# One weight load moved behind two others on the SP queue of a hybrid decoder layer

## The chip, the cores and the metric

The kernel runs on one core of a Trainium2 chip. The metric is the device time of one execution in microseconds (us), lower is better. The kernel before has a median of 944.97 us over 3 runs (944.78 to 945.34).

## The reference

One decoder layer over 1024 tokens and 16 meta tokens of width 1024, in float32. The change lies in the feed-forward part, at the seam where the mixing part ends:

```
h = h + rmsnorm(mix @ w_out, g_post_mix)
u = rmsnorm(h, g_pre_ffn)
f = square(relu(u @ w_ff1)) @ w_ff2        # w_ff1 1024 x 4096, w_ff2 4096 x 1024
h = h + rmsnorm(f, g_post_ffn)
```

## The kernel before, in words

All operands of a product are split into a high and a low float32r part, and a product is three matmuls (high by high, high by low, low by high: lines 125, 130 and 131). The high part is a cast on ACT (L96), the low part a subtraction on DVE (L99).

The first feed-forward product, `u @ w_ff1`, is done with fewer block products than the plain one, by sums of weight blocks and sums of token blocks. Its columns are cut into 16 blocks `p` of 256. For each block `prep_a(p)` loads two tiles of 512 KB, `r0` (the upper half of the rows of `w_ff1`) and `r1` (the lower half), makes sums of their quarters with `combine` (L1188, on DVE), and stores the changed `r1` to `s_dram` for later. For block 0, `r1` is a tile of the pool `d` (named d_3559 in the order of instructions) and `r0` one of the pool `raw` (raw_3557). Blocks 2 to 13 take `r1` from the pool `a`.

Four blocks of the upper and four of the lower rows are also loaded ahead of that, two at a time, by `early`: each call issues two loads of 256 KB (`w1_load`, L1185) and splits them. The last of these calls, `early(1, 2, ..., "a")`, loads the tile a_3494, casts it on ACT and subtracts on DVE. Its result is used by `p2(2, ...)` and `p2(3, ...)`, products into the bank `ps_pt`. `early` keeps the name of its second load in `loads[0]`.

The instructions of each engine are put in order by a scheduler when the kernel is built; `behind(name, ins)` adds an order without a wait: `ins` comes later in the stream than the instruction `name`. SP issues nearly all of these loads, and issues them in order: an issue that waits for its tile holds those behind it. Around the change the streams hold, besides: the last of the token rows (`out_norm`, `out_scale`, t = 7: squares on ACT at L1131, the root on POOL at L166 and L172, the scaling on DVE at L1143), their transposes on PE (L1157), and the sums of token blocks (`t_sums`), whose splits `ot2` are operands of the first products of block 0 (`product(ya[p], wa[p][1], ot2, False)`).

Of the kernel before, what the change touches and what calls it, by code (L numbers as in the profile page):

```python
# [37 lines left out]
def hybrid_layer(  # L38
# [19 lines left out]
    def slot(tag, shape, dt=F32):  # L58
        uid[0] += 1
        return slab.tile(shape, dt, tag=tag, name=f"{tag}{uid[0]}", bufs=bufs[tag])  # L60

    def pair(tag, shape):
        return slot(tag, shape, F32R), slot(tag, shape, F32R)
# [17 lines left out]
    def lut(*args, **kwargs):  # L81
        ins = nc.scalar.activation(*args, **kwargs).ins
        if last_lut[0] is not None:
            tc.add_manual_dep(
                ins, last_lut[0],
                mybir.DependencyInfo(
                    mybir.DependencyClass.NoSync, mybir.DependencyReason.DATA
                ),
                reason="lut",
            )  # L90
        last_lut[0] = ins.name
        return ins

    def split(hi, lo, src, eng=None):
        if eng is None:
            cast[0] = nc.scalar.copy(hi, src).ins.name  # L96
        else:
            eng.tensor_copy(hi, src)
        low = nc.vector.tensor_tensor(lo, src, f32(hi), op=ALU.subtract).ins  # L99
        mark[0] = low.name  # L100
        return low
# [4 lines left out]
    def behind(name, *inss):  # L106
        for ins in inss:
            tc.add_manual_dep(
                ins, name,
                mybir.DependencyInfo(  # L110
                    mybir.DependencyClass.NoSync, mybir.DependencyReason.DATA
                ),
                reason="order",
            )
# [924 lines left out]
    for half in range(2):  # L1039
        for c in range(NLRU):  # L1040
            y = ys[c][:, 512 * half : 512 * half + 512]
            ins = lut(y, y, AF.Gelu_apprx_tanh)
# [140 lines left out]
    def w1_load(dst, b, p, a0, a1):  # L1183
        c0 = 256 * p
        return nc.sync.dma_start(dst, w1v[b][:, :, c0 + P * a0 : c0 + P * a1]).ins  # L1185

    def combine(dst, x0, x1, op):
        return nc.vector.tensor_tensor(dst, x0, x1, op=op).ins  # L1188
# [25 lines left out]
    def prep_a(p, late=None):  # L1214
        r0 = slot("raw", [P, 4, 256])
        behind(loads[0], w1_load(r0, 0, p, 0, 2))
        r1 = slot("a" if 2 <= p < 14 else "d", [P, 4, 256])
        w1_load(r1, 1, p, 0, 2)
        a11, a21, a12, a22 = r0[:, :, LO], r0[:, :, HI], r1[:, :, LO], r1[:, :, HI]
        sums = [  # L1220
            combine(a22, a21, a22, ALU.add), combine(a21, a11, a21, ALU.subtract)
        ]
        if late:
            behind(late, *sums)
        hi, lo = pair("ws", [P, 4, 256])
        if p in a11_early:
            split(hi[:, :, HI], lo[:, :, HI], a21)
            first = a11_early[p]
        else:
            split(hi, lo, r0)  # L1230
            first = hi[:, :, LO], lo[:, :, LO]
        combine(a11, a22, a11, ALU.subtract)
        hl = slot("e", [P, 2, 4, P], F32R)
        split(hl[:, 0], hl[:, 1], a11)
        combine(a12, a12, a11, ALU.subtract)
        nc.gpsimd.dma_start(s_dram[p], r1)
        return first, (hl[:, 0], hl[:, 1]), (hi[:, :, HI], lo[:, :, HI])
# [9 lines left out]
    a11_early, a12_early, loads = {}, {}, [None]  # L1247
# [101 lines left out]
    product(y2, a12_early[1], b21, True, kcs=range(2))  # L1349
    t_sums(slice(8, 12))  # L1350
    wa[0] = prep_a(0)
    u2_tiles(7, xns[7])
    product(y2, a12_early[1], b21, True, turned[0], kcs=range(2, 4))
# [7 lines left out]
    for i in range(2):  # L1361
        behind(urgent, split(*map(rows, ot3[i]), t3[i]))
    token_low = mark[0]
    wa[1] = prep_a(1, urgent)


# [14 lines left out]
    for p in range(16):  # L1381
        if p + 2 < 16:
            wa[p + 2] = prep_a(p + 2, None if p else urgent)
        if p >= 13:
            raw_b[p - 13] = fetch_b(p - 13)
        product(ya[p], wa[p][1], ot2, False)
        nc.scalar.copy(block("12", p), ya[p])
        if p == 0:
            p2(3, a12_early[3], last_mm[0])
        if 4 <= p + 2 < 16:  # L1390
            p1(p + 2, wa[p + 2][0])
        product(ya[p], wa[p][2], ot3, False)
        nc.scalar.copy(block("21", p), ya[p])
        if 3 <= p < 9:
            t_rest(p - 3)

        if p == 14:
            ot1 = operand(u2f[1][0:2])
# [337 lines left out]
```

## Time and profile before

| what | value |
|---|---|
| median of 3 runs | 944.97 us (944.78 to 945.34) |
| profiled execution | 945.26 us, of which 943.3 us are the span from the first to the last instruction |
| mean granted TensorE clock | 0.999 of full speed |
| PE busy | 934.0 us, 99% of the span |
| DVE, ACT, POOL busy | 70%, 54%, 14% |
| DMA | 136.49 MB, mean 145 GB/s |
| stretch 311 to 345 us (around the change) | PE 34.00 us busy of 34, DVE 31.95, ACT 26.00, POOL 5.44 |

A row of the timeline has the start in us, the duration in us, the engine, the line, the operation, its tiles and in brackets the idle time ahead of it with what ended that. SPq rows are the issues of DMAs, not the transfers. The rows of the windows give the busy time of PE, of PE's weight load (PEld), of DVE, ACT and POOL, then the granted clock, the DMA share and GB/s.

### The profile page before, as it was taken

The numbers are of one execution on the slowest core, as the hardware profiler recorded it, in microseconds if no ns is written. First come the engines' busy times: TensorE is split into PE (matmuls) and PEld (weight loads), VectorE is DVE, ScalarE is ACT, GpSimd is POOL, SyncE is SP. The second block draws the span as 40 slices with busy tenths as digits, with TensorE's granted clock in tenths as the row PEclk, the third lists the DMA queues.
The fourth block names the chain that finished last, engine by engine and source line by source line (L and its number), as shares of the span: only waits on it lengthen the run. The fifth ranks groups of instructions, "written<-read, shape, count | busy, mean of one in ns | idle before, by whom it ended". The sixth has DMA issues, their size and how long they took to land.

```text
span 943.3 us, 12158 instructions
## 1 busy us (share of the span) xinstructions
PE 934.0 (99%) x4562; PEld 780.8 (83%) x4562; DVE 664.7 (70%) x846; ACT 505.1 (54%) x846; POOL 132.9 (14%) x204
## 2 busy tenths in 40 slices
PE   8999999999999999999999999999999999999997
PEld 7999999877888888888888888888888888888886
DVE  7667788889877986755544465477667676779794
ACT  8546765679434854443655575653533443445441
POOL 4104436430021200110000000001121000001200
PEclk9999999999999999999999999999999999999999
DMA  8220011104359768573422364334777755647934
GB/s 275 58 67 23 24 46 46 46 23 142 101 182 291 234 192 287 180 255 123 157 89 90 116 219 120 103 113 115 198 171 177 210 179 189 191 155 208 242 65 90
DMA packets 99911, 136.49 MB, mean 145 GB/s; under 512 B 24391, under 2 KB 63319, under 8 KB 99853
## 3 DMA queue, kind: packets, MB, share of 16 engines
q1 hardware_dynamic: 90652, 110.67, 36.7%
q0 software_dynamic: 8736, 23.67, 11.8%
q10 hardware_dynamic: 464, 1.38, 0.4%
q8 instruction: 36, 0.59, 0.3%
q14 instruction: 23, 0.18, 0.1%
HBM read 113.60 MB, written 21.50 MB: 143 GB/s over the span
## 4 chain that ended last, share of the span: by engine, by line
PE 98%; DVE 0%; DMA 0%; ACT 0%; issue 0%; DVEq 0%; ACTq 0%
PE ps_acc L125 12%; PE ps_acc L131 11%; PE ps_acc L130 11%; PE ps_pt L130 7%; PE ps_pt L125 7%; PE ps_pt L131 7%; PE ps_s L125 6%; PE ps_s L131 6%; PE ps_s L130 6%; PE ps_o L125 5%; PE ps_o L130 5%; PE ps_o L131 5%; PE ps_o L763 2%; PE ps_acc L988 1%; PE ps_acc L309 1%; PE ps_s L693 1%
## 5 line engine op out<-in xcount | busy, mean ns | idle before, releaser
L99 DVE TENSOR_TENSOR ws<-raw,ws 128x1024 fp32r<-128x1024 f32 (+1 forms) x69 | 83.6, 1212 | 74.3 <-ACT ws L96 23.3
L96 ACT CAST ws<-raw 128x1024 fp32r<-128x1024 f32 (+1 forms) x68 | 69.7, 1026 | 80.8 <-PE ps_o L130 32.6
L96 ACT CAST ws<-e 128x1024 fp32r<-128x1024 f32 x41 | 43.0, 1050 | 84.9 <-PE ps_o L130 37.8
L99 DVE TENSOR_TENSOR b<-b,b 128x1024 fp32r<-128x1024 f32 (+1 forms) x49 | 57.7, 1179 | 27.0 <-PE ps_o L130 21.7
L130 PE MATMUL ps_acc<-a,ws 128*128 128x512 f32 (+3 forms) x224 | 76.3, 341 | 0.0
L125 PE MATMUL ps_acc<-a,ws 128*128 128x512 f32 (+3 forms) x224 | 76.3, 341 | 0.0
L131 PE MATMUL ps_acc<-a,ws 128*128 128x512 f32 (+3 forms) x224 | 75.7, 338 | 0.0
L99 DVE TENSOR_TENSOR ws<-e,ws 128x1024 fp32r<-128x1024 f32 x41 | 50.2, 1224 | 31.2 <-ACT ws L96 17.8
L96 ACT CAST b<-b 128x1024 fp32r<-128x1024 f32 (+1 forms) x49 | 49.5, 1011 | 41.5 <-DVE b L1188 35.3
L750 POOL TENSOR_SCALAR_AFFINE_SELECT c<-c 128x512 fp32r<-128x512 f32 x64 | 51.4, 817 | 75.2 <-ACT c L96 66.1
L131 PE MATMUL ps_acc<-ws,b 128*128 128x512 f32 (+1 forms) x120 | 46.1, 384 | 0.0
L130 PE MATMUL ps_acc<-ws,b 128*128 128x512 f32 (+1 forms) x120 | 46.1, 384 | 0.0
L125 PE MATMUL ps_acc<-ws,b 128*128 128x512 f32 (+1 forms) x120 | 46.0, 385 | 0.0
L125 PEld LDWEIGHTS ps_acc<-a,ws 128*128 128x128 f32 x224 | 42.2, 188 | 3.1 <-DVE b L997 0.3
L131 PEld LDWEIGHTS ps_acc<-a,ws 128*128 128x128 f32 x224 | 42.2, 188 | 3.0
L130 PEld LDWEIGHTS ps_acc<-a,ws 128*128 128x128 f32 x224 | 42.1, 188 | 2.8
L130 PE MATMUL ps_pt<-ws,b 128*128 128x512 f32 x112 | 44.2, 395 | 0.0
L125 PE MATMUL ps_pt<-ws,b 128*128 128x512 f32 x112 | 44.2, 394 | 0.0
L131 PE MATMUL ps_pt<-ws,b 128*128 128x512 f32 x112 | 44.0, 393 | 0.0
L125 PE MATMUL ps_s<-ws,b 128*128 128x512 f32 x110 | 43.4, 395 | 0.0
L130 PE MATMUL ps_s<-ws,b 128*128 128x512 f32 x110 | 43.3, 393 | 0.0
L131 PE MATMUL ps_s<-ws,b 128*128 128x512 f32 x110 | 43.2, 393 | 0.0
(436 smaller groups left out, 2679.8 us busy)
## 6 DMA issues: line engine op xcount, KB each, us to landing
raw<-in_w_ff_dram SPq DMA_DIRECT2D x59, 512.0 KB
e<-in_w_ff_dram SPq DMA_DIRECT2D x43, 512.0 KB
a<-in_w_ff_dram SPq DMA_DIRECT2D x12, 512.0 KB
s_dram<-a POOLq DMA_DIRECT2D x12, 512.0 KB, 3.8
raw<-in_w_in_dram SPq DMA_DIRECT2D x9, 512.0 KB
c<-in_x_dram SPq DMA_DIRECT2D x8, 512.0 KB
d<-in_x_dram SPq DMA_DIRECT2D x8, 512.0 KB
out_dram<-raw SPq DMA_DIRECT2D x8, 512.0 KB
```

Source lines behind the costliest of these rows:

```text
L96: cast[0] = nc.scalar.copy(hi, src).ins.name
L99: low = nc.vector.tensor_tensor(lo, src, f32(hi), op=ALU.subtract).ins
L125: ins = nc.tensor.matmul(dst, lh, rh, start=start, stop=False, skip_group_check=True).ins
L130: nc.tensor.matmul(dst, lh, rl, start=False, stop=False, skip_group_check=True)
L131: last_mm[0] = nc.tensor.matmul(dst, ll, rh, start=False, stop=stop, skip_group_check=True).ins.name
L309: last_mm[0] = nc.tensor.matmul(acc[:, :n], w[k // 2][:, kc, :], u[kc][k % 2][:, t0 : t0 + n], start=k == 0 and kc == 0, stop=k == last an ...
L693: nc.tensor.matmul(dst, q[h][:, c], hi, start=True, stop=False, skip_group_check=True,)
L750: nc.gpsimd.affine_select(out=p_[:, :, s], in_=f32(p_[:, :, 0]), pattern=[[0, 4], [g, P]], compare_op=op, fill=0.0, base=0, channel_multip ...
L763: nc.tensor.matmul(two[:, :, oc : oc + w], v, p_.rearrange("p (j i) s c -> p j (i s c)", j=2)[:, :, pc : pc + w], start=n == 0 and k == 0, ...
L988: ins = nc.tensor.matmul(y2_bank[half], (wh, wh, wl)[k][:, kc, :], (uh, ul, uh)[k][:, t0 : t0 + n], start=m % 24 == 0, stop=m % 24 == 23, ...
```

## The change

In `prep_a`, the load of `r1` for block 0 is put behind `loads[0]`. When block 0 is prepared, that is the second load of the last `early` call. Until now only the load of `r0` was put there, and the scheduler had placed that of `r1` ahead of both early loads.

```diff
@@ prep_a
         r0 = slot("raw", [P, 4, 256])
         behind(loads[0], w1_load(r0, 0, p, 0, 2))
         r1 = slot("a" if 2 <= p < 14 else "d", [P, 4, 256])
-        w1_load(r1, 1, p, 0, 2)
+        ins = w1_load(r1, 1, p, 0, 2)
+        if p == 0:
+            behind(loads[0], ins)
```

On SP, in the stretch after the row of `out_dram` for t = 6, the difference is this (`d_3559` is `r1` of block 0, `a_3494` the early tile in two loads, `raw_3557` is `r0` of block 0):

```order
 L1087 DMA c_2787<-u_dram 128x4x64
 L1129 DMA out_dram<-raw_3333 128x1024
+L1185 DMA a_3494<-in_w_ff_dram 128x4x128 x2
 L1185 DMA d_3559<-in_w_ff_dram 128x4x256
-L1185 DMA a_3494<-in_w_ff_dram 128x4x128 x2
 L1185 DMA raw_3557<-in_w_ff_dram 128x4x256
 L1185 DMA a_3673<-in_w_ff_dram 128x4x256
```

The load of d_3559 now stands behind the two of a_3494, and still ahead of raw_3557. No other row of SP has moved.

On DVE, the instructions that use these loads, and those behind them, stand as before (d_3444 and raw_3446 are the token rows of t = 7):

```order
385 L1128 TENSOR_TENSOR raw_3446<-raw_3446,d_3444 128x1024
386 L99 TENSOR_TENSOR b_3443<-a_3439,b_3442 128x4x2x32
387 L99 TENSOR_TENSOR a_3493<-a_3494,a_3492 128x1024
388 L1188 TENSOR_TENSOR d_3559<-raw_3557,d_3559 128x4x128
389 L1143 TENSOR_SCALAR d_3444<-raw_3446,rs 128x1024
390 L1188 TENSOR_TENSOR raw_3557<-raw_3557 128x4x128
391 L1188 TENSOR_TENSOR a_3436<-c_2786,c_2784 128x256
```

Nothing moved there, nor on PE, ACT or POOL.

## The prediction

> **What bounds the kernel now.** I read the page's busy shares first, then the chain of waits, then who waited for whom on PE, then the windows and the timeline around the moved load.
>
> ```profile
> PE 934.0 (99%) x4562; PEld 780.8 (83%) x4562; DVE 664.7 (70%) x846; ACT 505.1 (54%) x846; POOL 132.9 (14%) x204
> PE 98%; DVE 0%; DMA 0%; ACT 0%; issue 0%; DVEq 0%; ACTq 0%
> PE ps_acc L339 <- DVE base_e L627: 1.5, 1, 1.5
> PE ps_o L401 <- DVE d L248: 1.0, 2, 0.8
> 311.00:345.00 34.00, 34.00 (x160) 27.69 (x159) 31.95 (x53) 26.00 (x54) 5.44 (x8) 1.00 0.63 199
> ```
>
> PE holds 98% of the chain that ended last. Its two waits on the list add up to 2.5 us, both at L339 and L401, which are the warm-up and the first transposes. In the stretch of the change, 311 to 345 us, it is busy for all of 34.00 us. The ends of PE's matmuls are modelled, so a small wait can lie inside a busy row; starts show it.
>
> ```profile
> 312.36 0.39 PE L130 MATMUL ps_acc<-b,a 128*128 128x512 f32 x1
> ...
> 317.47 0.39 PE L131 MATMUL ps_acc<-b,a 128*128 128x512 f32 x1
> ...
> 333.13 0.39 PE L131 MATMUL ps_pt<-b,a 128*128 128x512 f32 x1
> 333.36 0.40 PE L125 MATMUL ps_acc<-b,e 128*128 128x512 f32 x1
> ...
> 342.39 0.39 PE L130 MATMUL ps_s<-b,e 128*128 128x512 f32 x1
> 342.66 0.50 PE L131 MATMUL ps_acc<-b,e 128*128 128x512 f32 x1
> 342.99 0.40 PE L125 MATMUL ps_acc<-b,e 128*128 128x512 f32 x1
> ```
>
> From 312.36 to 317.47 there are 22 steps of 0.232 us each, and 0.23 us also lie between 333.13 and 333.36, where the first product with a weight made from the moved load begins (`e` is the high and low part of the first sum). So nothing waits there. At 342.39 the two steps are 0.27 and 0.33 us, 0.14 us above two regular ones: the one place near the change where PE can have been held up.
>
> **The change, part by part.** Nothing is added or removed; one issue of 512 KB moves behind two of 256 KB on SP. The issues before:
>
> ```profile
> 313.24 0.35 SPq L1129 DMA_DIRECT2D out_dram<-raw  x1
> 313.64 0.43 SPq L1185 DMA_DIRECT2D d<-in_w_ff_dram  x1
> 314.12 1.58 SPq L1185 DMA_DIRECT2D a<-in_w_ff_dram  x2
> 317.99 0.37 SPq L1185 DMA_DIRECT2D raw<-in_w_ff_dram  x1
> ```
>
> The three issues stand one behind the other from 313.64 to 315.70. They still will: the early loads begin at 313.64, and `d` goes out some 1.6 us later, by 315.7. The next issue, `raw`, went out at 317.99, with 2.3 us idle ahead of it. So nothing behind on SP moves, and the two early issues alone move ahead, by 0.48 us (314.12 - 313.64) plus the time that their bytes queued behind those of `d`. That second part is read from the bytes per microsecond:
>
> ```profile
> 314.00:315.00 1.00, 1.00 (x6) 0.82 (x5) 0.95 (x2) 1.00 (x4) 0.00 (x0) 1.00 0.95 365
> 315.00:316.00 1.00, 1.00 (x6) 0.82 (x5) 0.94 (x2) 1.00 (x6) 0.73 (x2) 1.00 0.91 206
> 316.00:317.00 1.00, 1.00 (x6) 0.79 (x5) 0.99 (x3) 0.92 (x4) 1.00 (x2) 1.00 0.97 273
> 317.00:318.00 1.00, 1.00 (x6) 0.82 (x5) 0.56 (x2) 1.00 (x2) 0.56 (x1) 1.00 1.09 359
> 318.00:319.00 1.00, 1.00 (x6) 0.81 (x5) 1.00 (x3) 1.00 (x3) 0.00 (x0) 1.00 1.15 314
> 319.00:320.00 1.00, 1.00 (x6) 0.81 (x5) 1.00 (x3) 0.47 (x1) 0.00 (x0) 1.00 0.70 163
> 320.00:321.00 1.00, 1.00 (x6) 0.81 (x5) 1.00 (x2) 0.89 (x1) 0.00 (x0) 1.00 1.07 375
> ```
>
> One GB/s over 1 us is 1 KB. The write of 524 KB (512 x 1024 bytes) is issued first, then `d`, `a`, `raw`, each 524 KB. In thousands of bytes the sum runs 365, 571, 844, 1203, 1517, 1680, 2055. If they move in the order of issue, the write ends at about 315.8, `d` (1049) at 317.6, `a` (1573) at 319.3 and `raw` (2097) at 321.1. These are estimates. ACT checks them:
>
> ```profile
> 318.85 0.62 ACT L96 CAST b<-a 128x512 fp32r<-128x512 f32 x1
> 320.11 1.05 ACT L96 CAST a<-a 128x1024 fp32r<-128x1024 f32 x1 [0.63 <-DMA a<-in_w_ff_dram]
> 321.06 1.06 ACT L1131 ACTIVATE d<-raw 128x1024 f32<-128x1024 f32 x1
> ```
>
> Its cast of the early tile began at 320.11, after 0.63 us of waiting for that load, which is 0.8 us after the estimated end of its bytes. With the same 0.8 us, the new order lands `a` at 317.6 + 0.8 = 318.4 and `d` at 319.3 + 0.8 = 320.1; `raw`, with the same bytes ahead of it, stays at 321.9.
>
> *The early tile.* ACT is free at 318.85 + 0.62 = 319.47, later than 318.4, so its wait of 0.63 us goes. What is late next is the square of the last token rows (L1131), which needs DVE's sum at L1128:
>
> ```profile
> 319.51 1.22 DVE L1128 TENSOR_TENSOR raw<-raw,d 128x1024 f32<-128x1024 f32 x1
> 321.25 1.22 DVE L99 TENSOR_TENSOR a<-a,a 128x1024 fp32r<-128x1024 f32 x1
> 322.39 0.69 DVE L1188 TENSOR_TENSOR d<-raw,d 128x512 f32<-128x512 f32 x1
> 322.29 0.86 POOL L166 TENSOR_SCALAR ms<-ssq 128x1 f32<-128x1 f32 x1 [4.74 <-ACT d L1131]
> 323.24 0.57 POOL L172 TENSOR_TENSOR rs<-ms,half_pow 128x1 f32<-128x1 f32 x1
> 323.84 0.75 DVE L1143 TENSOR_SCALAR d<-raw,rs 128x1024 f32<-128x1024 f32 x1 [0.77 <-POOL rs L172]
> ```
>
> That sum ends at 319.51 + 1.22 = 320.73, so the square starts 0.33 us earlier at best, and POOL's root and DVE's scaling with it: 0.33 of DVE's idle 0.77 us. DVE then runs nearly without a gap to the instructions that feed PE:
>
> ```profile
> 332.95 0.77 DVE L99 TENSOR_TENSOR b<-a,b 128x256 fp32r<-128x256 f32 x2
> 333.63 0.68 DVE L1308 TENSOR_TENSOR b<-ps_pt,b 128x512 f32<-128x512 f32 x1
> 341.91 0.69 DVE L99 TENSOR_TENSOR e<-raw,e 128x512 fp32r<-128x512 f32 x1
> ```
>
> L1308 adds a result of PE whose last matmul starts at 333.13 and ends at 333.52. DVE begins it at 333.63, so no more than 0.11 us of the 0.33 get past it, and the later `e` at 341.91, whose end (342.60) just precedes PE's 342.66, moves by 0.1 us. The gain at the end is therefore between nothing and the 0.14 us of the two long steps; I take 0.1, the share that passes L1308.
>
> *The moved load.* Its first reader is DVE's sum at 322.39, and that waits for `raw` too, which lands at 321.9 by the same estimate. `d` at 320.1 leaves 2.3 us to the sum and comes ahead of `raw` by 1.8. Cost: nothing, covered by the load of `raw`. If the cover fails and `d` lands after 322.39, DVE stands, with the scaling and the splits for PE's 333.36 behind it; PE had no slack there that I can show (the first of DVE's two splits from 332.95 ends at about 333.34, half of the 0.77 on), so each microsecond would be one at the end. Upper bound within the estimates: all four transfers share the engines and `d` ends with the last at 321.9, still 0.5 us ahead.
>
> A rule that stands against the estimate: the Trainium skill, "DMA: Bandwidth & Descriptors", section "Queues, rings and completion order", says that descriptors of a ring are consumed in order but that completion is not first in, first out. By it `d` could land after `raw`; the 0.63 us of ACT agree with the order of issue, and no run here shows the other case.
>
> *Sum.* The profiled execution took 945.26 us (943.3 of span, 1.96 around it), 0.29 above the median. From its own time the change takes 0.1, to 945.16; from the median, 944.87, rounded to 944.9.
>
> **The rivals.**
>
> *The freed waits reach the end (faster).* If PE's even steps hide waits, the most that this change frees is ACT's 0.63 plus DVE's 0.77 = 1.40 us, giving 943.57; with ACT's alone, 944.34. For it: DVE is busy 31.95 of 34 us and feeds PE to within 0.02 us at 333.36. Against it: PE's steps are as even there as at 312 to 317. Even all of it stays below 0.2% of the time, which is 1.89 us, about what a measurement of this kernel can tell from no change. The Trainium skill's "Perfetto Trace Analysis", section "Identifying the Most-Contended Engine", holds matmul busy time to be a poor measure of headroom and points to the weight load's; by that 34.00 - 27.69 = 6.31 us of this stretch would be open (an estimate), but this trace's even starts don't agree.
>
> *A wait of SP takes hold of the moved issue (slower).* `d` is now the last of three, and SP also waits for older transfers before issues:
>
> ```profile
> SPq L1185 <- DMA out_dram<-raw: 5.0, 3, 2.6
> ```
>
> If `d`'s issue waits w longer than the 315.7 reckoned, `d` lands at 320.1 + w, and `raw`, issued behind it, as much as 1.8 us after that. DVE's sum at 322.39 is then late by 320.1 + w + 1.8 - 322.39 = w - 0.5. It decides from w = 0.5 and passes 0.2% from w = 2.4. At the longest such wait, 2.6 us, the time is 944.97 + 2.1 = 947.1; at all three together, 5.0 us, 949.5. Against it: whatever stood ahead of the third issue before stands there now, and that one was out by 315.70.
>
> *It does not do what it says.* The row of SP has changed, but if the transfers share the engines rather than follow each other, the early tile lands about as before: 944.97.
>
> **How the numbers follow.** Forecast (0.1 us or none) 0.87; freed waits reaching the end 0.06; SP's wait 0.05; shared transfers 0.02. Over 0.2% faster would need more than the 1.40 us that can come free: 0.02, out of the second case. Over 0.2% slower: 0.04 of the third. Within: 0.94. The range: from the fastest run less ACT's wait, 944.78 - 0.63 = 944.1, to the slowest plus a small SP wait (w = 1.6), 945.34 + 1.1 = 946.4.
>
> **What would show it.** In the profile after, the two `a` issues stand first at about 313.6 and `d` third at about 315.2; ACT's wait of 0.63 us for `a` is gone and L1131 starts near 320.75; DVE's wait ahead of L1143 falls from 0.77 to about 0.45; the sum at 322.39 does not move; PE stays at 34.00 of 34 us. I am wrong if DVE waits for a DMA ahead of that sum, if SP has a wait ahead of `d`, or if PE's steps around 333.36 or 342.66 lengthen.

## The result, and the profile after

The changed kernel takes 946.92 us (median of 19 runs, 945.78 to 949.15) where the kernel before takes 945.12 in the same runs: a ratio of 1.0018, 95% interval 1.0012 to 1.0024. So it is some 1.8 us slower. Its profiled execution is one of its quicker ones, 945.99 us with a span of 944.0, which is 0.73 us over the profiled execution of before. (The ratios are estimates of their own, given with their interval, and can differ a little from the quotient of two medians.)

First the page's busy line and chain, then the new line among PE's waits (in us: total, times, longest), then the window from 311 to 345 us:

```profile
PE 934.7 (99%) x4562; PEld 780.8 (83%) x4562; DVE 664.6 (70%) x846; ACT 505.2 (54%) x846; POOL 134.6 (14%) x204
PE 97%; DVE 1%; ACT 0%; DMA 0%; issue 0%; DVEq 0%; ACTq 0%
```

```profile
PE ps_acc L125 <- ACT b L96: 0.2, 1, 0.2
```

```profile
311.00:345.00 34.00, 33.76 (x157) 27.02 (x156) 32.25 (x54) 26.11 (x54) 5.32 (x8) 1.00 0.62 194
```

DVE has come into the chain with 1%, PE has a third wait, and PE is busy for 33.76 of the 34.00 us in which it was busy throughout. Three matmuls fewer fit there (157 for 160). SP's issues in the timeline (here and below, rows that lie between those shown are left out):

```profile
313.91 0.35 SPq L1129 DMA_DIRECT2D out_dram<-raw  x1
314.31 1.32 SPq L1185 DMA_DIRECT2D a<-in_w_ff_dram  x2
315.73 0.63 SPq L1185 DMA_DIRECT2D d<-in_w_ff_dram  x1
318.05 0.37 SPq L1185 DMA_DIRECT2D raw<-in_w_ff_dram  x1
```

The order is the intended one, and `raw` goes out at 318.05, where before had 317.99. The timeline of ACT, then of DVE, where these loads are used:

```profile
319.44 1.04 ACT L96 CAST a<-a 128x1024 fp32r<-128x1024 f32 x1
321.43 1.06 ACT L1131 ACTIVATE d<-raw 128x1024 f32<-128x1024 f32 x1 [0.94 <-DVE raw L1128]
```

```profile
320.18 1.22 DVE L1128 TENSOR_TENSOR raw<-raw,d 128x1024 f32<-128x1024 f32 x1
321.92 1.22 DVE L99 TENSOR_TENSOR a<-a,a 128x1024 fp32r<-128x1024 f32 x1
324.17 0.69 DVE L1188 TENSOR_TENSOR d<-raw,d 128x512 f32<-128x512 f32 x1 [1.03 <-DMA raw<-in_w_ff_dram]
324.78 0.75 DVE L1143 TENSOR_SCALAR d<-raw,rs 128x1024 f32<-128x1024 f32 x1
```

ACT's cast of the early tile has no wait in brackets any more. But the first sum of block 0 now waits 1.03 us for a load, and that load is not the one that was moved: it is `raw`, whose place on the queue is the same. The sum starts at 324.17 instead of 322.39. Ten microseconds later, on DVE and then on PE:

```profile
332.99 0.75 DVE L1188 TENSOR_TENSOR a<-a,c 128x256 f32<-128x256 f32 x2
333.88 0.77 DVE L99 TENSOR_TENSOR b<-a,b 128x256 fp32r<-128x256 f32 x2
```

```profile
333.26 0.40 PE L131 MATMUL ps_pt<-b,a 128*128 128x512 f32 x1
333.90 0.50 PE L125 MATMUL ps_acc<-b,e 128*128 128x512 f32 x1 [0.24 <-ACT b L96]
334.36 0.50 PE L130 MATMUL ps_acc<-b,e 128*128 128x512 f32 x1
334.70 0.39 PE L131 MATMUL ps_acc<-b,e 128*128 128x512 f32 x1
334.93 0.40 PE L125 MATMUL ps_acc<-b,e 128*128 128x512 f32 x1
```

DVE's splits start at 333.88, before they did at 332.95: still 0.93 us late. PE needs 1.67 us from 333.26 to 334.93, four steps that take 0.93 at 0.232 each. The 0.74 lost there is about the whole difference of the two profiled times. The 0.24 in brackets is only part of it: the rest hides in longer rows, since PE's ends are modelled.

So the two ends of the chain are clear, and the experiments have two questions: is DVE's wait what costs the time, and why does `raw` come late.

### The profile page after: what moved, and what is told of

Read it like the earlier page. It is cut to its first block, busy times and chain, and to the rows that moved or that the text cites. A ratio compares the mean times of both kernels' runs of the same rounds, so it can differ in the third digit from the quotient of the medians.

```text
span 944.0 us, 12158 instructions
## 1 busy us (share of the span) xinstructions
PE 934.7 (99%) x4562; PEld 780.8 (83%) x4562; DVE 664.6 (70%) x846; ACT 505.2 (54%) x846; POOL 134.6 (14%) x204
## 3 DMA queue, kind: packets, MB, share of 16 engines
q10 hardware_dynamic: 464, 1.38, 0.5%
## 4 chain that ended last, share of the span: by engine, by line
PE 97%; DVE 1%; ACT 0%; DMA 0%; issue 0%; DVEq 0%; ACTq 0%
PE ps_acc L125 12%; PE ps_acc L130 11%; PE ps_acc L131 11%; PE ps_s L125 6%; PE ps_s L130 6%; PE ps_s L131 6%; PE ps_pt L130 6%; PE ps_pt L125 6%; PE ps_pt L131 6%; PE ps_o L125 5%; PE ps_o L130 5%; PE ps_o L131 5%; PE ps_o L763 2%; PE ps_acc L988 1%; PE ps_acc L309 1%; PE ps_s L693 1%
```

## The experiments

The theories. **A**: `raw` lands late, DVE runs in order, PE gets its operands late. For why `raw` is late: **F**, PE's fetch of its instructions (a 16 KB transfer about every 28 us) meets this load; **C**, the two loads of 512 KB read the same columns of `w_ff1` and get in each other's way; **S**, two loads with wide rows stand directly one behind the other; **T**, there is no spare time between the end of the load ahead and that of `raw`, so a DMA engine that lags does not catch up.

In kernels with added lines the sum L1188 is L1190, L1192 or L1193.

### Both kernels once more

No edit.

> The changed kernel once more. Theory A (late block): the two loads of block 0 land later than DVE can use them, because the moved load now lies directly ahead of raw_3557 in the queue and a lagging DMA engine has no gap in which to catch up. Expected: DVE's sum of block 0 again waits for a DMA, starts past 323.5 us, and PE loses 0.5 to 3 us at the first product of block 0 near 333.4 us; time 946 to 948. Rival B (chance): the late landing of the first profile was one engine's bad luck and the time comes from elsewhere; then the sum starts near 322.4 and PE's loss lies at another place.

> The kernel before once more, for a second profile. Theory A: the sum of block 0 starts without a DMA wait near 322.4 us, PE regular at 333.4; time 945.0. Rival B: the landing of raw_3557 scatters as much as in the changed kernel, with a wait of DVE for it of 1 us or more possible.

The changed kernel: 946.77 us, ratio to before 1.0019 [1.0009, 1.0028]. The kernel before: 945.47, 1.0002 [0.9993, 1.001]. The waits and PE's timeline of the changed one:

```profile
DVE d L1188 <- DMA raw<-in_w_ff_dram: 1.8, 1, 1.8
```

```profile
333.21 0.40 PE L131 MATMUL ps_pt<-b,a 128*128 128x512 f32 x1
334.32 0.50 PE L125 MATMUL ps_acc<-b,e 128*128 128x512 f32 x1 [0.71 <-ACT b L96]
```

It took 946.70, 0.71 more than the first profile of this kernel. DVE's wait is 0.8 longer in it, and PE's step is 1.11 instead of 0.64: the loss grows with the wait. The kernel before was not as theory A expected it, with no wait, but as the rival did: in this second profile of it (945.78), DVE's sum waited 0.52 us, `raw` ended at 323.63 instead of 321.71, and PE's four steps at 333 us lost 0.54 (334.48 - 333.01 less 0.93), where in the first profile they lost nothing. The late load is thus no property of the changed kernel alone.

### Taking work off DVE behind the late load

In both kernels a split and the sum for `s_dram`, which PE doesn't need soon, go behind the last urgent split:

```diff
-            split(hi[:, :, HI], lo[:, :, HI], a21)
+            low = split(hi[:, :, HI], lo[:, :, HI], a21)
-        combine(a12, a12, a11, ALU.subtract)
+        last_sum = combine(a12, a12, a11, ALU.subtract)
+        if p == 0:
+            lazy.extend((low, last_sum))
...
+    behind(urgent, *lazy)
```

> The changed kernel, with two DVE instructions of block 0 that PE does not need before 338.9 us (the low part of ws, and the sum that goes to s_dram; 0.6 us each) put behind the last of the four splits that PE needs at 333.4. Theory A: the loads land as late as before but DVE has 1.2 us in hand, so most of the 1.8 us come back: 945.2 to 946.0. Rival B, and any rival in which the loss is not on DVE's path to 333.4: no gain, 946.5 to 947.3.

> The kernel before with the same two DVE instructions put back. Theory A: DVE's 1.2 us in hand take away what scatter the kernel before had: 944.7 to 945.1, with a narrower spread. Rival: the moved instructions come late for PE at 338.9 or for s_dram, 945.5 or more.

A miss for A, which expected 945.2 to 946.0 and 944.7 to 945.1. With the change 947.52, 1.0026 [1.0017, 1.0035]; before with the same edit 945.78, 1.0006 [0.9997, 1.0015]. The waits with the change:

```profile
DVE d L1188 <- DMA raw<-in_w_ff_dram: 2.2, 1, 2.2
PE ps_acc L131 <- DVE e L99: 1.6, 1, 1.6
PE ps_acc L125 <- ACT b L96: 0.3, 1, 0.3
```

PE's steps at 333 us in the same profile:

```profile
332.95 0.40 PE L131 MATMUL ps_pt<-b,a 128*128 128x512 f32 x1
333.60 0.49 PE L125 MATMUL ps_acc<-b,e 128*128 128x512 f32 x1 [0.26 <-ACT b L96]
334.74 0.39 PE L125 MATMUL ps_acc<-b,e 128*128 128x512 f32 x1
```

The place at 333 us is not cured: the four steps lose 0.86 (334.74 - 332.95 less 0.93), and the 0.3 of the list is only what shows as idle. How much the edit spared there can't be told, since DVE's wait was longer here (2.2). And PE now waits 1.6 at 342.6 for the next operand of DVE (`e`, 0.6 in before with this edit, so that part of this wait comes from the edit itself): work that is taken from in front of one deadline stands in front of the next. The places of the loss fit A, but this pair does not decide for it. Moving these two operations is no remedy.

### PE's fetch of instructions

The profile lists one DMA queue with 36 transfers of instructions and 0.59 MB, 16 KB each. Fifty tiny matmuls in place of a part of the warm-up shift PE's count of instructions, so that the fetch falls at 314.1 us, away from `raw`; the start takes some 3 us longer. In a third kernel eight of them put it inside the transfer of `raw`, in the kernel before.

```diff
-    load(11, 512)
+    load(5, 512)
+    for _ in range(50):
+        nc.tensor.matmul(
+            idle[:16, :16], zeros[:16, :16], zeros[:16, :16], start=True, stop=True,
+            skip_group_check=True,
+        )
```

> The changed kernel with PE's stream of instructions shifted: 6 of the 11 warm-up matmuls at the start give way to 50 tiny ones, so that the transfer that fetches PE's instructions (16384 B, near 322.4 us in every profile so far, in the middle of the loads of block 0) comes some 10 us earlier, near 312 us, where the DMA queues are empty. Theory F (the fetch holds up one DMA engine while it carries raw_3557): raw_3557 lands by 322.5 us on all engines, DVE waits less than 0.3 us, PE loses under 0.3 us at the first product of block 0; the time is that of fetch_before to within 0.3 us, 944.5 to 946.0. Theory S (two wide loads one behind the other, rows of 1024 B without the two narrow loads between them, leave engines behind): as slow against fetch_before as the changed kernel against the kernel before, 1.3 to 2.3 us.

> The kernel before with the same shift, as the base for fetch_after. Both theories: 944.5 to 945.8 us, PE regular at 333.4 (shifted with the start); under theory F with less scatter than before, since now and then the fetch reaches raw_3557 there too.

> The kernel before with the fetch of PE's instructions moved 1.6 us earlier, into the transfer of raw_3557 (one warm-up matmul gives way to 8 tiny ones). Theory F: raw_3557 lands at 323 us or later on one engine, DVE's sum of block 0 waits 0.7 to 2 us, PE loses 0.5 to 1.5 us near 333.4; 945.7 to 947. Theory S: no change, 944.7 to 945.5.

With the change 949.58, 1.0046 [1.0032, 1.0059]; before with the same shift 947.76, 1.0024 [1.0014, 1.0034]. The difference is 1.82 us, as without the shift, and the wait is there without a fetch at `raw`:

```profile
DVE d L1193 <- DMA raw<-in_w_ff_dram: 1.7, 1, 1.7
```

Before with the fetch put at `raw`: 945.48, 1.0009 [1.0001, 1.0018]; DVE's sum came 1 us later:

```profile
323.44 0.69 DVE L1193 TENSOR_TENSOR d<-raw,d 128x512 f32<-128x512 f32 x1 [0.91 <-PE ps_o L1162]
```

(PE's work at L1162 was long done; the load ended at 323.35.) Wait and landing are as F expected, the time is in the other range. A fetch may hold up a load (one profile), but the changed kernel is as late without one: F falls as the cause of the difference. What it adds in single profiles comes up with the landings.

### Other columns, narrower loads

`other_cols` lets the moved load read the columns of block 5, so that block 0's product is of wrong weights. `halves` and `halves_again` issue the moved load as two of half the row width, `upper_halves` does so with `raw`.

```diff
# other_cols
-        ins = w1_load(r1, 1, p, 0, 2)
+        ins = w1_load(r1, 1, p or 5, 0, 2)
# halves, halves_again
...
+            for c in range(2):
+                ins = w1_load(r1[:, :, P * c : P * c + P], 1, p, c, c + 1)
# upper_halves
...
+            for c in range(2):
+                upper = w1_load(r0[:, :, P * c : P * c + P], 0, p, c, c + 1)
```

> The changed kernel with the moved load of 512 KB issued as two of 256 KB, rows of 512 B as in the early loads, in the same place of SP's order. Theory S: raw_3557 lands by 322.5 us as in the kernel before, and the time comes back to 945.0 to 945.5. Theory F: no change, 946.3 to 947.3.

> The kernel with the moved load in two halves once more, for a second profile and a narrower interval; its first profile showed one engine 2.3 us behind on raw_3557 and the first time lay between the two kernels. Theory S: the two engines that lag in every profile of the changed kernel don't lag here, and what was left is a fetch of PE's instructions on one engine; 945.3 to 946.3. Theory C: half of the moved load still lies beside raw_3557, so a lag of about half the size stays, 945.7 to 946.7.

> The changed kernel, in which the moved load reads the columns of block 5 in place of those of block 0 (so block 0's sums are made from another block's lower half); size, place and every instruction are as in the changed kernel. Theory C (the moved load and raw_3557, now adjacent, read the same columns of rows that lie 8 MiB apart in HBM and hinder each other): raw_3557 lands by 322.5 us on all engines, time 945.0 to 945.8. Theory S (adjacent loads with rows of 1024 B, whatever they read): two engines still land raw_3557 1.5 us or more behind the median, time 946.3 to 947.3.

> The changed kernel, with raw_3557 in place of the moved load issued as two loads of 256 KB with rows of 512 B. Theory S: no two wide loads are adjacent, the tile lands by 322.5 us on all engines, 945.0 to 945.8. Theory C: the same rows and columns of HBM are read side by side as before, 946.3 to 947.3.

Other columns: 947.02, 1.0016 [1.0007, 1.0024], as slow as the change; C is not borne out. Its profile caught its quickest execution (945.29), with `raw` on time. Halves: 946.13, 1.0009 [1.0001, 1.0018], and a second time 946.89, 1.0017 [1.0006, 1.0028]. The halves of `raw`: 946.19, 1.0011 [1.0002, 1.002]. Row widths are inconclusive: the three times lie outside all the ranges that were expected, DVE's wait is 1.4 in the first of these profiles, absent in the second, 0.8 in the third, and the 12 executions of `halves_again` fall into five at 945.0 to 945.3 and seven at 946.6 to 950.6 (three of the seven at a granted clock of 0.994 to 0.997, where the others have 0.998 or 0.999). The profiles of `halves` and `halves_again`, and the two of before, show that the same program meets the late load in one execution and not in another.

These kernels also answer the first question, whether DVE's wait costs the time. In `other_cols`, `halves_again` and `upper_halves` the instructions of DVE, ACT and POOL around the change stand as in the changed kernel. DVE's sum and PE's steps in `other_cols`:

```profile
322.97 0.68 DVE L1188 TENSOR_TENSOR d<-raw,d 128x512 f32<-128x512 f32 x1
333.35 0.39 PE L131 MATMUL ps_pt<-b,a 128*128 128x512 f32 x1
333.58 0.40 PE L125 MATMUL ps_acc<-b,e 128*128 128x512 f32 x1
334.28 0.40 PE L125 MATMUL ps_acc<-b,e 128*128 128x512 f32 x1
```

With the changed order and `raw` on time, PE's four steps take 0.93 and the execution is as quick as those of before. The five profiles in order of DVE's wait for `raw` (us):

| profile | DVE's wait | lost in PE's four steps | this execution |
|---|---|---|---|
| `other_cols` | 0 | 0.00 | 945.29 |
| `halves_again` | 0 | 0.02 | 945.25 |
| `upper_halves` | 0.8 | 0.59 | 945.46 |
| changed kernel | 1.0 | 0.74 | 945.99 |
| changed kernel again | 1.8 | 1.21 | 946.70 |

The loss grows with the wait and is gone without it. A is borne out.

### The moved load, earlier

`d_first` keeps the order of before and issues `d` ahead of the write of the token rows of t = 6; `a_first` keeps the order of the change and issues the early tile ahead of that write. There `d` still stands directly in front of `raw`, but goes out at 313.95 instead of 315.73.

```diff
# d_first
-            behind(loads[0], ins)
+            behind(ins.name, outs[6])
...
# a_first
-            behind(loads[0], ins)
+            behind(loads[0], ins, outs[6])
+            behind(outs[6].name, ins)
+            behind(ins.name, upper)
...
```

(The lines left out keep the write of the last token rows behind other loads, the last square behind ACT's cast of the early tile, and the sums of block 0 behind its split. A few more instructions of DVE and ACT stand otherwise.)

> The order of the kernel before, with the moved load issued one place earlier still: ahead of the write of out for t = 6, near 312.3 us, where the DMA queues are empty (a few instructions past 325 us stand otherwise too, the scheduler's choice). Theory T (raw_3557 is late on one or two engines where there is no spare time between the loads ahead of it and its own start): all bytes ahead of raw_3557 are through by 318.7, a gap opens, it lands by 322 us on all engines; 944.4 to 945.1, the best of all, with less scatter than before. Theory S (only what lies directly ahead counts, and the two narrow loads do not harm): as the kernel before, 944.8 to 945.5.

> The changed kernel, with its two early loads issued ahead of the write of out for t = 6, so that everything up to raw_3557 moves about 1 us earlier while the moved load stays directly ahead of raw_3557 (here too a few instructions stand otherwise, DVE's scaling ahead of the first sum among them). Theory T: the gap is there, raw_3557 lands by 322.3 us, no wait of DVE for it over 0.3 us; 944.6 to 945.4. Theory S: the adjacent wide loads leave engines behind as in the changed kernel; DVE waits 0.7 us or more for raw_3557, 945.8 to 947.

The time: 946.85, 1.0016 [1.0007, 1.0025], and 946.33, 1.001 [1.0001, 1.0018]. Neither has a wait of DVE for `raw`, whose load has ended by 321.92 in the one and 321.59 in the other (the landings stand below): the lateness is gone, and the time is not back; T had expected 944.4 to 945.1 and 944.6 to 945.4. The waits and DVE's timeline of `a_first`, then the waits of `d_first`, say why:

```profile
PE ps_acc L130 <- DVE b L99: 0.7, 1, 0.7
```

```profile
333.60 0.69 DVE L1323 TENSOR_TENSOR b<-ps_pt,b 128x512 f32<-128x512 f32 x1 [0.54 <-PE ps_pt L131]
```

```profile
DVE b L1316 <- PE ps_pt L131: 0.7, 1, 0.7
PE ps_acc L130 <- DVE b L99: 0.9, 1, 0.9
```

The scheduler has put the addition of a result of PE (L1308 in the kernel before) in front of the splits for PE's next product. DVE waits for PE there, and PE then for DVE. That is a second cost, which is not a wait for the load.

### The same with that addition held, and a pause ahead of `raw`

Two kernels hold that addition behind both splits; some other instructions of DVE still stand otherwise than in the kernel before, most of them in `a_first_held`. `gap` puts three tiny stores on SP between `d` and `raw` in the changed kernel, so that `raw` is issued 1.3 us later; `gap_again` is the same once more. Here too the scheduler has moved some of DVE's instructions: the addition stands between the two splits.

```diff
# d_first_held, a_first_held
+        added[p] = nc.vector.tensor_tensor(
+            block("11", p), y2, block("11", p), op=ALU.add
+        ).ins
...
+    behind(urgent, added[2])
# a_first_held also
...
+            behind(sums[0].name, scaled_7[0])
+            behind(scaled_7[0].name, sums[1])
# gap, gap_again
...
+            for k in range(3):
+                ins = nc.sync.dma_start(pause_dram[k], xns[6][:, 0:16]).ins
...
```

> The changed kernel with three tiny stores on SP between the moved load and raw_3557, which wait for what raw_3557's issue waits for, so raw_3557 is issued about 1 us later and the engines have emptied (8 KB each to a scratch tensor; a few of DVE's instructions stand otherwise). Theory T: the lag of single engines goes although the load is issued later; it lands on all engines at 322.3 to 323 us, and the time falls to 945.2 to 946.2. Theory S or a plain queue: the load is 0.7 to 1 us later still, 947 to 948.

> gap a second time, with no edit. Spare time (T): 945.2 to 946.2, VectorE's wait for raw under 1.0 though raw is issued 1.3 us later. A plain queue or adjacency (S): 947 to 948, the later issue adding its 1.3 us to the wait.

> The moved load before the early tiles and the last row write, as in d_first, with VectorE's addition of p2(2) kept behind the last urgent split, so that VectorE's order is the one of the kernel before. Spare time (T): the load of raw has 1.3 us or more ahead of it, lands by 322.4, no wait of VectorE for it, steps of PE even at 333.4: 944.5 to 945.2. If the order of VectorE was not what cost d_first 1.7 us: 946.5 to 947.0, with a wait of PE at L130 near 0.9 again.

> The order of the changed kernel (early tiles, then the moved load directly ahead of raw) with all three ahead of the last row write, and VectorE's order held as in the kernel before. Spare time (T): raw lands on all engines by 322.4, 944.6 to 945.5. Adjacency of the two wide loads (S): VectorE waits for raw 0.7 or more, 946 to 947.

`d_first_held`: 945.32, ratio 1.0 [0.9992, 1.0008]. `a_first_held`: 945.79, 1.0001 [0.9993, 1.001]. `gap`: 945.81, 1.0009 [1.0001, 1.0018]; `gap_again`: 945.96, 1.0002 [0.9994, 1.0011]. The first two lie a little above T's ranges and well below the ranges of the rivals; `a_first_held` is still 0.42 above the median of before in the same rounds (945.37), but its 12 executions lie between 945.58 and 946.21, those of the changed kernel between 945.78 and 949.15. With the pauses the times are in the range that T gave, and `raw` ends 0.6 to 0.7 past the 323.0 that T gave at most. From the timeline of `a_first_held`, SP's issues, DVE's sum and PE's step:

```profile
314.12 0.38 SPq L1189 DMA_DIRECT2D d<-in_w_ff_dram  x1
317.88 0.37 SPq L1189 DMA_DIRECT2D raw<-in_w_ff_dram  x1
322.81 0.68 DVE L1192 TENSOR_TENSOR d<-raw,d 128x512 f32<-128x512 f32 x1
333.19 0.40 PE L131 MATMUL ps_pt<-b,a 128*128 128x512 f32 x1
333.62 0.49 PE L125 MATMUL ps_acc<-b,e 128*128 128x512 f32 x1
```

The two wide loads stand one behind the other as in the change, and the sum starts at 322.81 with no wait: S falls as a cause that is enough by itself. The early tile goes out ahead of them here, and the time between their issues is 3.8 us instead of 2.3. PE's step is 0.43 instead of 0.64. Its four steps still lose 0.54 (0.30 in `d_first_held`): DVE's splits wait 0.4 us for ACT here. The same of `gap_again`:

```profile
319.31 0.38 SPq L1185 DMA_DIRECT2D raw<-in_w_ff_dram  x1
323.68 0.69 DVE L1188 TENSOR_TENSOR d<-raw,d 128x512 f32<-128x512 f32 x1 [0.89 <-DMA raw<-in_w_ff_dram]
333.47 0.44 PE L125 MATMUL ps_acc<-b,e 128*128 128x512 f32 x1
```

Issued 1.26 us later than in the changed kernel, `raw` is there 0.5 us earlier (323.56 for 324.04; the loads ahead were issued 0.35 earlier in this execution). A queue in which bytes simply follow each other would not do that. DVE's wait of 0.89 stays, and PE's four steps lose 0.27; as DVE's order differs too, what the pauses gain in time is not the load's alone.

### What the landings say

Each of these loads is reported done by 16 DMA engines. The table is worked out from the trace's records of those reports. "Spare" is the time from the last report of the load ahead of `raw` to the eighth or ninth report (their mean) of `raw`; "lag" is from there to its last one.

```
kernel                 load ahead, last   raw, half   raw, last   spare    lag
a_first                     318.30         321.26      321.59      2.96    0.33
a_first_held                318.41         321.27      321.54      2.86    0.27
gap_again                   320.40         322.84      323.56      2.44    0.72
gap                         320.71         322.90      323.71      2.19    0.81
d_first_held                319.93         321.81      322.09      1.88    0.28
d_first                     319.63         321.39      321.92      1.76    0.53
fetch_before                323.05         324.61      324.81      1.56    0.20
before                      320.08         321.46      321.71      1.38    0.25
fetch_hit_before            320.19         321.41      323.35      1.22    1.94
path_before                 320.19         321.39      322.00      1.20    0.61
path_after                  321.00         322.11      325.27      1.11    3.16
halves                      322.63         323.70      326.34      1.07    2.64
again_before                320.70         321.72      323.63      1.02    1.91
fetch_after                 323.71         324.52      327.33      0.81    2.81
after                       321.09         321.79      324.04      0.70    2.25
again_after                 320.67         321.37      324.46      0.70    3.09
other_cols                  321.00         321.70      322.61      0.70    0.91
halves_again                321.25         321.78      322.52      0.53    0.74
```

(`upper_halves`, where `raw` is two loads, is left out; in `gap` the tiny stores are not counted as a load.) Half of the engines are done with `raw` at 321.3 to 322.1 in all profiles in which it was issued by 318.4, the change included: what is late is the last engines. With 1.38 us of spare time or more the last engine is never over 0.81 behind, in 8 profiles of 8; with less it is 1.9 to 3.2 behind in 7 of 10. The bound of 1.38 is read off this table afterwards, and nearly every kernel has a single profile in it.

How much spare time the change took is less clear. In the first two profiles it is 0.7 us (1.38 to 0.70), but that execution of the changed kernel started these transfers 0.67 us later, as the second profile of before did (0.73), which has 1.02 and the lag too. Against that one the change took 0.32. Nor is "spare" independent of the lag: in the changed kernel the load ahead is already drawn out, its last engine 0.87 and 0.94 behind its half in the two profiles, against 0.39 and 0.36 in those of before.

Fetches have a part in it that the table does not show. With the order of before, the two lags over 1.9 are those where the trace has PE's fetch start inside the load of `raw`: at 320.95 in `fetch_hit_before`, where it was put, and at 321.62 in `again_before`. In the other three it starts at 322.49, 323.08 and 314.09, and the lag is 0.2 to 0.61. (The expectations had it near 322.4 in every profile so far, but in `path_after` it was at 320.55.) So a lack of spare time need not be what made those two late, though a fetch at that place does not always harm (`d_first_held`: 321.61, lag 0.28). With the changed order the lag is there without a fetch: in `fetch_after` three engines were over 2.7 behind, with the fetch at 314.08. In the two profiles of the changed kernel it starts at 322.36 and 322.33, while their last engines were still at work; what it added there stays open.

What speaks for T are the kernels that were given spare time on purpose: in six profiles none has a lag over 0.81. T is borne out as a condition: with spare time no long lag was seen, without it one can happen. That the moved load ends later in this place than the early tile did is not its size alone, since cut in two it ended at 321.25 (`halves_again`); this stays open. Which engine lags, and why in one execution and not in the next, stays open: the reports don't name the engine. (The Trainium skill, "DMA: Bandwidth & Descriptors", section "Latency and other measured facts", calls two of the 16 usually slower, with a cause that it calls uncertain and ties to GpSimd's queue; no run here can show whether these are the ones.)

No kernel beat the one before: `d_first_held`, the best, equals it.

## Why the prediction was wrong

**The step that failed** is "`raw`, with the same bytes ahead of it, stays at 321.9", and with it the cover of the moved load ("Cost: nothing, covered by the load of `raw`"). The byte sum gives one time for a load. For half of the engines it was good: `raw` 321.79 against 321.9, `d` 320.22 against 320.1, the early tile 318.63 against 318.4 (closer by some luck, since the issues came 0.67 us later than reckoned; in the second profile it is 321.37, 319.72 and 318.26). But a load is over when the last of its engines is, and for `raw` that was 324.04, 2.1 us later (`d` 321.09, 1.0 later). The 0.8 us put on top of the byte sum came from one wait in one execution, in which the engines of that load ended within 0.4 us of each other (half at 319.70, the last at 320.08). DVE was free at 321.92 + 1.22 = 323.14, so the wait is 1.03.

**The bound from the other side was too narrow.** "All four transfers share the engines and `d` ends with the last at 321.9" bounds `d` and takes the last end as fixed. Nothing quoted bounded that end from above.

**No slack at 333.36: right.** "Each microsecond would be one at the end" was written for `d`, and held in the main for `raw`: 0.93 us of lateness on DVE, 0.74 on PE, and the loss grew with the wait in five profiles of one order. The sum is 1.78 late: 0.75 because DVE itself came later in this execution (323.14 for 322.39), 1.03 by the wait. The idle 0.77 ahead of L1143 would have taken up the 0.75; with the wait it is used up, and L1143 starts 0.94 late (324.78 for 323.84). Two of the signs that the prediction named for being wrong are there: DVE waits for a DMA ahead of that sum, and PE's steps around 333.36 are longer.

**ACT's wait of 0.63: right that it goes, wrong that it could be seen as a gain.** The cast starts at 319.44. The square expected near 320.75 starts at 321.43, because DVE's sum at L1128 starts 0.67 late; the write of the rows of t = 6 (313.91 for 313.24), which is issued ahead of the moved loads, is late by the same 0.67, so this comes from further up in that execution. The gain of 0.1 us was not to be seen.

**SP: right.** The issues stand as expected, the third at 315.73 for 315.2 where everything on SP is 0.67 later, and `raw` at 318.05 for 317.99. The rival of a wait of SP did not come in, though its ending did: the sum late, by another way.

**The rule on completion.** The loads did not end out of order: in each of the 18 profiles the load ahead of `raw` ended first, so `d` never came after `raw`, as the prediction had held possible by it. What the prediction lacked is beside that rule. The Trainium skill, "DMA: Bandwidth & Descriptors", section "Why a DMA increments its semaphore by 16 and not by 1", says that only the full count of the engines means that the data has landed. The trace agrees: 15 of 16 had reported `raw` by 322.38, and DVE started at 324.17, 0.13 after the last at 324.04.

**The size of an effect.** The time, 946.92, lies past the upper end of 946.4, which was put together from SP's wait alone. The freed waits had no share in the result, and the change did what it says.

## What to carry to other kernels

Where a load's first reader has little slack, ask for the end of its slowest DMA engine, not for the sum of the bytes ahead: a load with the same bytes ahead of it ended later here when another load took the place right in front of it, by 2.3 us in the first pair of profiles (324.04 for 321.71) and by 0.8 in the second (324.46 for 323.63). Look at what is queued next to a moved transfer, even where the transfer itself has time to spare, and give an urgent load some time to itself (here 1.4 us from the end of the load ahead to the time at which half of its own engines were done). Profile the same program more than once before calling a landing late: the kernel before had a late one too. When a fix takes the wait away and the time stays, compare the order of the waiting engine's instructions before dropping the theory: here the scheduler had traded one loss for another.

## What the runs showed of the hardware that was not expected

- Of the 16 DMA engines that share a load of 512 KB, one to five were over 1 us behind the half in 7 of 18 profiles, the last by 1.9 to 3.2 us, in one execution and not in the next of the same program. With 1.38 us or more of spare time ahead of it this was not seen (0.2 to 0.8).
- A load issued 1.3 us later can land 0.3 to 0.5 us earlier (323.71 and 323.56 for 324.04).
- Instructions come in by DMA too, 16 KB at a time; where PE's fetch was put inside the load of `raw`, the last engine ended at 323.35, with half of them done at 321.41 (one profile; in `again_before`, with the fetch at 321.62, it was 323.63 and 321.72).
